# State space stage of an even layer: wide rotations by pairs of tiles, sums on TensorE, gates ahead of the attention heads, output projection between them

## The chip, the cores and the metric

The kernel runs on one core of a Trainium2 chip. The metric is the device time in microseconds (us). Before the change it is 1637.96 us, the median of three runs (1635.64 to 1639.87). TensorE (PE in the profile, its weight loads PEld) multiplies matrices into PSUM, VectorE (DVE), ScalarE (ACT) and GpSimd (POOL) work element by element, and SyncE (SP) issues the weight transfers.

## The reference, cut to what matters

A first block of two layers (feed-forward, a mixer of three branches, feed-forward) is followed by a second block: an even layer and an odd layer. The change lies in the even layer. All data are float32, 256 tokens, width 1024.

```python
h = rms_norm(x, even_norm_g)
q, k, v, z_a, u, z_b = split(h @ even_w_in)           # 4 x 1024 and 2 x 512 columns
q, k = per-head rms_norm(q), per-head rms_norm(k)     # 8 heads of 128
o_a = stick_breaking_attention(q, k, v) * silu(z_a)
o_b = s5_mixer(u, ...) * silu(z_b)
x = x + concatenate([o_a, o_b]) @ even_w_out          # 1536 x 1024

def s5_mixer(u):     # 32 groups of 16 channels, 64 complex states each
    bu = B_bar u                                      # real and imaginary
    h[t] = lam_bar h[t-1] + bu[t]                     # complex, diagonal
    y = C_re h.real - C_im h.imag + d u
    y = gelu(y)
    return y * sigmoid(y @ w_glu + b_glu)

def stick_breaking_attention(q, k, v):                # s < t
    z = q k / sqrt(128)
    w[t, s] = exp(log_sigmoid(z) + sum over s < j < t of (log_sigmoid(z) - z)[t, j])
    return w v
```

## The kernel before, in words

Activations lie transposed: 128 channels on the partitions, 256 tokens along the free axis (T = 256). Products of float32 matrices with weights are made in three parts: `W` (line 298 fetches, 311 and 312 split) takes a weight half of 128 x 1024, rounds it to a short form `wh` on ScalarE (L311) and has VectorE compute the rest `wl` (L312); `mm3` (L317 to L319) then multiplies wh x hi, wh x lo and wl x hi. `proj` runs that over the chunks of the contraction; for 1024 channels it is 24 matmuls of 256 columns. `tokens` gives token-major results in four steps of 12 matmuls of 512 columns each (L624 to L626). Two weight halves form a pair of 1 MB that one transfer on SyncE's queue brings; four buffers `raw` hold pairs, six buffers `hl` hold split halves.

`even` begins with the projection of u and the norm's factors. After that it holds three kinds of work. The first is a list `fills` of 36 closures: 24 token steps for v, q and k (the groups end in `heads`' norms, L1097 to L1102, and, three steps later, transposes, L1113), then twelve gates, 8 to 11 (z_b) ahead of 0 to 7 (z_a). `fill(x)` takes x of them on average, with the remainder carried over. Gates 8 to 11 get silu by a tanh at once, gates 0 to 7 by one activation after the last head (L1286).

The second is the state space part, 16 tiles of 128 states. `states(i)` makes the real and imaginary input products (L1160, L1161; 32 contraction rows, another group of 32 rows for each of four tiles) in one PSUM bank, then rotates them into the frame of the state: four VectorE products with the tables cos and sin (L1164, L1165, L1167, L1168) and two GpSimd sums (L1166, L1169). `rotate(i)` scans both parts along the tokens (L1177, L1178) and rotates back: two products on VectorE (L1180, L1183), two on GpSimd (L1181, L1184) and two GpSimd sums (L1182, L1185). `output(i)` makes two products with C (L1192, L1193; 32 output columns) into a quarter of one of two banks held for the whole part. `activated(c)` adds d u to four tiles' results and applies gelu. The loop runs over 18 steps with 1.4 fills each: `states(i + 1)`, `rotate(i)`, `output(i - 2)`. The GLU follows: four products of 12 matmuls.

The third is the attention: for each head `logits` (L1235), `remainder` (L1252) and `attend` (L1267), each with passes on ScalarE, VectorE and GpSimd between, one step apart over ten steps with one fill each. Then come silu of the z_a gates, the final norm's factor into new chunks (L1290), the product of heads and gates (L1294), and the output projection `out_rows`: twelve chunks of 24 matmuls, accumulated in four PSUM banks, added to h at the end (L1299).

The order on each engine is made by a scheduler ahead of the run from the order in which the code gives the work; buffers go back to their pools when all readers are done. PSUM has two banks each under the names a and b and four under c; temporaries have 12 buffers of 384 columns.

Of the kernel before, what the change touches and what calls it, by code (L numbers as in the profile page):

```python
# [9 lines left out]
F32 = mybir.dt.float32  # L10
# [20 lines left out]
# ---------------------------------------------------------------- host layout  # L31
# [204 lines left out]
# -------------------------------------------------------------------- kernel  # L236


class Kern:
    def __init__(self, ctx, tc, a, sizes, vwhere, cwhere):  # L240
# [7 lines left out]
        self.rawp = pool("raw", 4)  # L248
# [14 lines left out]
    # ---- small helpers  # L263
# [72 lines left out]
    def pair(self, n):  # L336
        """hi and lo accessors over n chunks of [P, T]."""
# [14 lines left out]
    def bcast(self, col, ps=None):  # L352
        """[P, 2] token columns -> [P, T] rows on every partition."""
# [13 lines left out]
    def token_sum(self, sq, st=None):  # L367
        """Columns [P, 2]: the sum of sq over partitions, per token."""
# [40 lines left out]
    def out_rows(self, tag, ks, ys, evac):  # L409
        """T-layout output, contraction chunk outermost; the last two by bank."""  # L410
        acc = [self.psc() for _ in range(4)]
        n = len(ks)
        done = {}
# [6 lines left out]
        for k in range(n - 2):  # L420
# [3 lines left out]
        ws = [self.W(tag + str(k)) for k in ks[n - 2:]]  # L424
        for b in range(4):
            for i in range(2):
                for d in (2 * b, 2 * b + 1):
                    blk(ws[i], n - 2 + i, d)
            for d in (2 * b, 2 * b + 1):
                evac(d, acc[b][:, (d % 2) * T:(d % 2) * T + T])  # L430
# [6 lines left out]
    # ---- parts  # L437
    def setup(self, x=True):
# [10 lines left out]
        # the tensor engine's clock rises while it works: it starts before the data come  # L449
# [10 lines left out]
    def setup_pos(self):  # L460
        """Distances and rotation tables from the positions: closures."""
# [6 lines left out]
        def fetch():  # L468
# [3 lines left out]
            pi = t["i"] = self.tp.tile([P, 384], I32, tag="t", name="posi")  # L472
# [31 lines left out]
    def reduce_angle(self, eng, y, x, k):  # L504
        """y = x - 2 pi round(x / 2 pi), within [-pi, pi]."""
# [7 lines left out]
    def ffn(self, part, l, h, extra=()):  # L513
# [13 lines left out]
        def project(f, *ups):  # L527
# [8 lines left out]
            # both at once: they follow the norm's chunks  # L536
# [53 lines left out]
    def small_norm(self, cks, g, n):  # L590
        """rmsnorm of T-layout chunks cks, then split."""
# [19 lines left out]
    def tokens(self, names, xs, sink, tag="a"):  # L611
        """Token-major [P, 512] per token block, contraction over 1024: four closures."""
# [44 lines left out]
    def pv(self, ptb, o, v, h):  # L657
        """o[qb][:, h*64:+64] = P @ v for both query blocks."""
# [6 lines left out]
    def attention(self, scores, pes, fill, pv, begun=0):  # L665
        """Scores, transposes and products of the eight heads, one stage apart."""
# [18 lines left out]
    def to_chunks(self, o, ys, scale=None):  # L685
        """token-major o [P, 2, 512] -> split T-layout chunks."""
# [11 lines left out]
    def mix(self, part, l, h):  # L698
# [10 lines left out]
        # latent attention: compressed inputs  # L709
# [16 lines left out]
        # differential attention inputs  # L726
# [17 lines left out]
        # lambda of the differential attention, on every partition  # L744
# [10 lines left out]
        # latent attention inputs  # L755
# [42 lines left out]
        def branch(n, c, ys):  # L798
            """Chunks c and c + 1 of branch n, gated, into the sum."""
# [64 lines left out]
        # latent attention  # L864
# [16 lines left out]
        # differential attention; o comes out times the first map's row sum  # L881
# [651 lines left out]
```

## Time and profile before

| what | before |
|---|---|
| median of three runs | 1637.96 us (1635.64 to 1639.87) |
| span of the profiled execution | 1638.3 us, mean granted TensorE clock 0.992 |
| TensorE busy, matmul / weight load | 1593.0 / 1501.5 us |
| VectorE / ScalarE / GpSimd busy | 1086.4 / 823.2 / 488.0 us |
| state space products on TensorE | first input product at 1280.67 us |
| attention heads | first logits at 1425.0 us |
| output projection of the even layer | last sum starts at 1506.6 us |

The busy time of an engine is the time in which at least one of its instructions runs; the records of matmuls overlap, so the busy time of weight loads says better how densely TensorE is fed. A group's line gives the count, the busy time, the mean of one instruction in ns, and the idle time ahead of it with what ended it.

### The profile page before, as it was taken

Reading aid. Unit: us, or ns where it says so; the run is one execution under the profiler, and the core shown is the slowest. Engines: PE = TensorE matmul, PEld = TensorE weight load, DVE = VectorE, ACT = ScalarE, POOL = GpSimd, SP = SyncE. Lnnn points to the kernel's source line nnn. Section 1 sums busy time; section 2 is a strip of 40 time slices with the busy share of each in tenths; the row PEclk is TensorE's granted clock in tenths of the full one; section 3 lists DMA queues with packets and bytes.
Section 4 is the critical chain, followed back from the end, with each engine's and each line's share of the span. In section 5 each row is a group of like instructions: output and inputs, shape, how many; then the busy total and the mean of one; then the engine's idle time right before and its main releaser. Section 6 shows DMA issues by size and latency. Waiting matters only on the chain.

```text
span 1638.3 us, 29940 instructions
## 1 busy us (share of the span) xinstructions
PE 1593.0 (97%) x12182; PEld 1501.5 (92%) x12182; DVE 1086.4 (66%) x1781; ACT 823.2 (50%) x1409; POOL 488.0 (30%) x539
## 2 busy tenths in 40 slices
PE   8999999999999999999999999999999989899998
PEld 8999998999999999999998999999999756789876
DVE  6655676676765557555576576776667899866642
ACT  5444455554544445444455564544545243575662
POOL 4111232003321113111142002455453678422232
PEclk9999999999999999999999999999999999999999
DMA  8555543344455554555544344554445322323520
GB/s 308 191 187 177 186 168 129 129 155 155 155 205 181 181 180 180 181 180 180 183 164 149 130 149 153 181 183 167 173 156 181 128 103 103 129 104 133 187 93 26
DMA packets 38313, 261.47 MB, mean 160 GB/s; under 512 B 4320, under 2 KB 5600, under 8 KB 7200
## 3 DMA queue, kind: packets, MB, share of 16 engines
q1 hardware_dynamic: 37440, 257.67, 44.4%
q8 instruction: 95, 1.56, 0.4%
q0 software_dynamic: 592, 1.81, 0.4%
q14 instruction: 42, 0.34, 0.1%
q10 hardware_dynamic: 144, 0.08, 0.0%
HBM read 258.50 MB, written 1.05 MB: 158 GB/s over the span
## 4 chain that ended last, share of the span: by engine, by line
PE 73%; DVE 13%; POOL 8%; issue 3%; ACT 3%; DMA 0%; SPq 0%; DVEq 0%; ACTq 0%; POOLq 0%
PE psa L317 11%; PE psa L318 11%; PE psa L319 11%; PE psc L318 6%; PE psc L319 6%; PE psc L317 6%; PE psb L317 5%; PE psb L318 4%; PE psb L319 4%; DVE wl L312 4%; POOL t L571 2%; POOL t L984 1%; ACT wh L311 1%; POOL t L822 1%; DVE s L334 1%
## 5 line engine op out<-in xcount | busy, mean ns | idle before, releaser
L312 DVE TENSOR_TENSOR wl<-raw,wh 128x1024 fp32r<-128x1024 f32 (+1 forms) x487 | 610.3, 1260 | 226.2 <-ACT wh L311 223.1
L311 ACT ACTIVATE wh<-raw 128x1024 fp32r<-128x1024 f32 (+1 forms) x487 | 505.8, 1049 | 423.0 <-PE psa L318 193.4
L317 PE MATMUL psa<-s,wh 128*128 128x256 f32 x1800 | 517.3, 288 | 1.4 <-ACT s L333 0.6
L318 PE MATMUL psa<-s,wh 128*128 128x256 f32 x1800 | 512.5, 285 | 3.9 <-DVE s L334 3.6
L319 PE MATMUL psa<-s,wl 128*128 128x256 f32 x1800 | 511.0, 284 | 0.0
L317 PEld LDWEIGHTS psa<-s,wh 128*128 128x128 f32 x1800 | 345.3, 192 | 11.1 <-issue 4.6
L318 PEld LDWEIGHTS psa<-s,wh 128*128 128x128 f32 x1800 | 345.5, 192 | 9.7 <-DVE s L334 7.8
L319 PEld LDWEIGHTS psa<-s,wl 128*128 128x128 f32 x1800 | 345.0, 192 | 2.2 <-issue 1.9
L571 POOL TENSOR_TENSOR t<-t,hrb 128x256 f32<-128x256 f32 x88 | 117.7, 1338 | 489.7 <-ACT t L570 489.7
L319 PE MATMUL psb<-s,wl 128*128 128x256 f32 x752 | 213.0, 283 | 1.1 <-DVE wl L312 1.1
L317 PE MATMUL psb<-s,wh 128*128 128x256 f32 x752 | 213.6, 284 | 0.0
L318 PE MATMUL psb<-s,wh 128*128 128x256 f32 x752 | 212.8, 283 | 0.0
L317 PE MATMUL psc<-hs,wh 128*128 128x256 f32 x704 | 198.7, 285 | 6.6 <-ACT hs L330 6.6
L318 PE MATMUL psc<-hs,wh 128*128 128x256 f32 x704 | 200.5, 286 | 1.5 <-DVE hs L331 1.0
L319 PE MATMUL psc<-hs,wl 128*128 128x256 f32 x704 | 199.2, 284 | 0.0
L319 PEld LDWEIGHTS psb<-s,wl 128*128 128x128 f32 x752 | 144.3, 192 | 1.5 <-DVE wl L312 1.5
L317 PEld LDWEIGHTS psb<-s,wh 128*128 128x128 f32 x752 | 144.3, 192 | 0.4 <-ACT t L1224 0.2
L318 PEld LDWEIGHTS psb<-s,wh 128*128 128x128 f32 x752 | 144.3, 192 | 0.0
L317 PEld LDWEIGHTS psc<-hs,wh 128*128 128x128 f32 x704 | 134.6, 192 | 8.3 <-ACT hs L330 8.2
L318 PEld LDWEIGHTS psc<-hs,wh 128*128 128x128 f32 x704 | 135.6, 193 | 3.5 <-DVE hs L331 3.5
L319 PEld LDWEIGHTS psc<-hs,wl 128*128 128x128 f32 x704 | 135.6, 193 | 0.0
L330 ACT ACTIVATE hs<-t 128x256 fp32r<-128x256 f32 x88 | 36.7, 417 | 156.0 <-DVE t L572 155.9
(366 smaller groups left out, 2323.6 us busy)
## 6 DMA issues: line engine op xcount, KB each, us to landing
raw<-in_w SPq DMA_DIRECT2D x242, 1024.0 KB, 4.8
s<-in_x SPq DMA_DIRECT2D x4, 256.0 KB, 5.1
raw<-in_w SPq DMA_DIRECT2D x4, 256.0 KB, 5.7
out<-t SPq DMA_DIRECT2D x8, 128.0 KB, 1.8
cst<-in_cst SPq DMA_DIRECT2D x1, 609.5 KB, 12.5
sq<-in_pw POOLq DMA_DIRECT2D x2, 256.0 KB, 3.7
s<-in_s5b POOLq DMA_DIRECT2D x1, 512.0 KB, 3.7
s<-in_s5c POOLq DMA_DIRECT2D x1, 512.0 KB, 3.9
```

What stands on the lines that cost most here:

```text
L311: self.act = nc.scalar.activation(hi[:, s], src[:, s], AF.Copy)
L312: nc.vector.tensor_tensor(lo[:, s], src[:, s], hi[:, s].bitcast(F32), ALU.subtract)
L317: mm(ps, wh, xh, start=start, stop=False, skip_group_check=True)
L318: mm(ps, wh, xl, start=False, stop=False, skip_group_check=True)
L319: return mm(ps, wl, xh, start=False, stop=stop, skip_group_check=True)
L330: nc.scalar.activation(hi, src, AF.Copy)
L334: nc.vector.scalar_tensor_tensor(lo, src, scale, hi.bitcast(F32), ALU.mult, ALU.subtract)
L571: nc.gpsimd.tensor_tensor(sg, sg, hrb, ALU.mult)
L822: nc.gpsimd.tensor_tensor(dst[:, 16:16 + T], src[:, 16:16 + T], src[:, 16 - sh:16 - sh + T], ALU.add)
L984: g.tensor_tensor(u, u, w, ALU.subtract)
```

## The change

State space tiles go in pairs. `states(n)` makes the input products of two tiles in turn, in two banks; each tile's real and imaginary part are then multiplied as one operand of 512 columns by cos and by sin, so two VectorE products take the place of four; the two GpSimd sums stay, in place. `rotate(n)` scans in place and makes two products of 512 columns on VectorE; the four GpSimd operations go. `output(n)` makes four products per tile instead of two, with a negated copy of the first matrix (`cneg`, made once in the preparation), so that TensorE's accumulation does the sums; the two tiles of a pair alternate. The loop has ten steps with 2 x 1.6 fills. All gates get silu by the tanh, and all fills left are done ahead of the GLU. The heads write into the projection's operands directly: the gate is multiplied on the way out of PSUM, the factor 0.5 is in the split. The final norm's factor is applied to h in place ahead of the heads. The output projection is cut into steps; they stand between the heads, without one in the loop's step 3. Its accumulators are the four banks c, and the heads' products use banks a and b. For the wider temporaries (512 columns) the weight buffers `raw` go from four to three, for the whole kernel.

```diff
-        self.rawp = pool("raw", 4)
+        self.rawp = pool("raw", 3)
...
-        t = self.tp.tile([P, 384], dt, tag="t", name="t")
+        t = self.tp.tile([P, 512], dt, tag="t", name="t")
...
+    def out_steps(self, tag, ks, ys, evac):
...
+        def step(k):
+            if not acc:
+                acc.extend(self.psc() for _ in range(4))
             w = self.W(tag + str(ks[k]))
             for d in range(8):
                 blk(w, k, d)
...
+            cn = self.const.tile([P, 16, 32], F32, name="cneg")
+            g.tensor_scalar(cn, c0[:, 0], -1.0, None, ALU.mult)
+            self.cp = c0[:, 0], c0[:, 1], cn
...
-            if c >= 8:
-                t = self.tmp()
-                nc.scalar.activation(t, z, AF.Tanh, scale=0.5)
-                nc.vector.scalar_tensor_tensor(z, t, 1.0, z, ALU.add, ALU.mult)
+            t = self.tmp()
+            nc.scalar.activation(t, z, AF.Tanh, scale=0.5)
+            nc.vector.scalar_tensor_tensor(z, t, 1.0, z, ALU.add, ALU.mult)
...
+        def states(n):
+            ii = (2 * n, 2 * n + 1)
+            pb = [self.psc() for _ in ii]
+            for m in range(2):
+                for i, ps in zip(ii, pb):
+                    r = slice(32 * (i % 4), 32 * (i % 4) + 32)
+                    nc.tensor.matmul(ps[:, m * T:m * T + T], bm[r, i // 4, m], u[r, i // 4],
+                                     start=True, stop=True)
+            for i, ps in zip(ii, pb):
+                gc, gs = self.tmp(512), self.tmp(512)
+                nc.vector.tensor_tensor(pairs(gc), pairs(ps), table(self.cos(i)), ALU.mult)
+                nc.vector.tensor_tensor(pairs(gs), pairs(ps), table(self.sin(i)), ALU.mult)
+                nc.gpsimd.tensor_tensor(gc[:, 0:T], gc[:, 0:T], gs[:, T:512], ALU.add)
+                nc.gpsimd.tensor_tensor(gc[:, T:512], gc[:, T:512], gs[:, 0:T], ALU.subtract)
+                hst[i] = gc, gs
+
+        def rotate(n):
+            for i in (2 * n, 2 * n + 1):
+                gc, gs = hst[i]
+                rho = self.rho[:, i:i + 1].to_broadcast([P, T])
+                for s in (slice(0, T), slice(T, 512)):
+                    nc.vector.tensor_tensor_scan(gc[:, s], rho, gc[:, s], 0.0, ALU.mult, ALU.add)
+                nc.vector.tensor_tensor(pairs(gs), pairs(gc), table(self.sin(i)), ALU.mult)
+                nc.vector.tensor_tensor(pairs(gc), pairs(gc), table(self.cos(i)), ALU.mult)
+
+        def output(n):
+            cr, ci, cn = self.cp
+            c = n // 2
+            for k, (m, src, half) in enumerate(((cr, 0, 0), (ci, 0, 1), (ci, 1, 0), (cn, 1, 1))):
+                for i in (2 * n, 2 * n + 1):
+                    o = yps[c % 2][32 * (i % 4):32 * (i % 4) + 32, (c // 2) * T:(c // 2) * T + T]
+                    nc.tensor.matmul(o, m[:, i], hst[i][src][:, half * T:half * T + T],
+                                     start=k == 0, stop=k == 3, skip_group_check=True)
...
+        for n in range(10):
+            fill(1.6)
+            if n < 7:
+                states(n + 1)
+            fill(1.6)
+            if n < 8:
+                rotate(n)
+            if 0 < n < 9:
+                output(n - 1)
+            if n > 1 and n % 2 == 0:
+                activated(n // 2 - 1)
...
+        fill(len(fills))
+        for c in range(4):
+            glu(c)
...
-            pz = self.psc()
+            pz = self.psa("a")
...
-            pr = self.psc()
+            pr = self.psa("b")
...
-            nc.scalar.activation(oa[hd // 4][:, hd % 4], po[:, 0:T], AF.Copy)
+            t = self.tmp()
+            nc.vector.tensor_tensor(t, po[:, 0:T], za[hd // 4][:, hd % 4], ALU.mult)
+            ys = ysa[hd // 4]
+            self.split(ys[0](hd % 4), ys[1](hd % 4), t, scale=0.5)
...
+        rfb = self.bcast(rf, self.psa("b", T))
+        for k in range(8):
+            nc.vector.scalar_tensor_tensor(h(k), h(k), self.v("final_norm", k), rfb, ALU.mult, ALU.mult)
...
-        for hd in range(10):
-            fill(1.0)
+        for hd in range(9):
             if hd < 7:
                 logits(hd + 1)
+            if len(steps) > 1 and hd != 3:
+                steps.pop()()
             if hd < 8:
                 remainder(hd)
+            if len(steps) > 1 and hd > 3:
+                steps.pop()()
-            if 0 < hd < 9:
+            if hd > 0:
                 attend(hd - 1)
```

## Rows read from the trace of the kernel before

**Rows 1.** The page: busy us, share of the span, instructions.

```profile
PE 1593.0 (97%) x12182; PEld 1501.5 (92%) x12182; DVE 1086.4 (66%) x1781; ACT 823.2 (50%) x1409; POOL 488.0 (30%) x539
```

**Rows 2.** Busy time by stage: stretch, its length, busy us (instructions), clock, DMA.

```profile
core 0: us, PE busy (x) PEld busy (x) DVE busy (x) ACT busy (x) POOL busy (x), PEclk, DMA share, GB/s
1282.00:1410.00 128.00, 115.19 (x472) 77.88 (x471) 121.22 (x178) 46.21 (x99) 105.99 (x103) 0.95 0.27 94
1475.00:1490.00 15.00, 15.00 (x127) 15.00 (x127) 10.94 (x13) 7.78 (x11) 3.15 (x4) 1.00 0.38 141
```

**Rows 3.** Groups by line, 1282 to 1410 us, VectorE: busy us, mean ns.

```profile
L312 DVE TENSOR_TENSOR wl<-raw,wh 128x1024 fp32r<-128x1024 f32 x24 | 38.3, 1634 | 0.0
...
L1183 DVE TENSOR_TENSOR t<-t,s 128x256 f32<-128x256 f32 x16 | 14.1, 878 | 0.0
...
L1164 DVE TENSOR_TENSOR t<-psc,s 128x256 f32<-128x256 f32 x16 | 6.6, 412 | 2.0 <-PE psc L1161 2.0
...
L1102 DVE TENSOR_TENSOR sq<-psa,sm 128x512 f32<-128x512 f32 x4 | 2.7, 684 | 0.1
```

**Rows 4.** The same view, 1410 to 1515 us, VectorE and ScalarE.

```profile
L312 DVE TENSOR_TENSOR wl<-raw,wh 128x1024 fp32r<-128x1024 f32 x26 | 31.5, 1224 | 15.7 <-ACT wh L311 15.6
...
L1241 ACT ACTIVATE t<-t,cst 128x384 f32<-128x384 f32 x8 | 4.9, 614 | 0.2
```

**Rows 5.** VectorE and GpSimd in order of time: start us, duration us, instruction.

```profile
1293.25 0.68 DVE L1177 TENSOR_TENSOR_SCAN t<-s5p,t 128x256 f32<-128x256 f32 x1
1293.85 1.16 DVE L1178 TENSOR_TENSOR_SCAN t<-s5p,t 128x256 f32<-128x256 f32 x1
...
1300.78 0.72 POOL L1166 TENSOR_TENSOR t<-t 128x256 f32<-128x256 f32 x1
...
1304.87 1.71 POOL L1182 TENSOR_TENSOR t<-t 128x256 f32<-128x256 f32 x1
...
1305.91 0.41 DVE L1164 TENSOR_TENSOR t<-psc,s 128x256 f32<-128x256 f32 x1
1306.25 0.41 DVE L1165 TENSOR_TENSOR t<-psc,s 128x256 f32<-128x256 f32 x1
...
1310.15 1.75 DVE L312 TENSOR_TENSOR wl<-raw,wh 128x1024 fp32r<-128x1024 f32 x1
1311.83 0.41 DVE L1164 TENSOR_TENSOR t<-psc,s 128x256 f32<-128x256 f32 x1
```

**Rows 6.** One line's instructions: ns min/median/max, first and last start.

```profile
L1183 DVE TENSOR_TENSOR t<-t,s x16: 413/948/965, 1289.4 to 1402.5; 128x256 f32<-128x256 f32 x16
```

**Rows 7.** TensorE in order of time, state space stretch.

```profile
1279.21 0.39 PE L624 MATMUL psb<-wh,s 128*128 128x512 f32 x1
...
1279.89 0.39 PE L624 MATMUL psb<-wh,s 128*128 128x512 f32 x1
...
1280.67 0.69 PE L1160 MATMUL psc<-s 32*128 32x256 f32 x2
1281.20 0.59 PE L1161 MATMUL psc<-s 32*128 32x256 f32 x2
...
1296.46 0.62 PE L1192 MATMUL psc<-t,s 128*32 128x256 f32 x2
...
1297.44 0.50 PE L624 MATMUL psa<-wh,s 128*128 128x512 f32 x1
```

**Rows 8.** TensorE in order of time, differential attention of the first layer.

```profile
366.01 0.61 PE L646 MATMUL psb<-s 32*128 32x256 f32 x4
```

**Rows 9.** Weight buffers: two stretches in order of time, and all fetches' landing.

```profile
444.62 5.16 DVE L312 TENSOR_TENSOR wl<-raw,wh 128x1024 fp32r<-128x1024 f32 x4
...
451.93 1.06 ACT L311 ACTIVATE wh<-raw 128x1024 fp32r<-128x1024 f32 x1 [2.25 <-PE psb L318]
...
DMA to landing us min/median/max: 4.0/4.8/11.6
```

**Rows 10.** One line's instructions, first logits and last sums.

```profile
L1235 PE MATMUL psc<-s x16: 377/379/383, 1425.0 to 1462.0; 128*128 128x256 f32 x16
...
L1299 DVE TENSOR_TENSOR s<-psc,s x8: 407/414/425, 1502.1 to 1506.6; 128x256 f32<-128x256 f32 x8
```

More of the change, by code (lines that the diff above doesn't have):

```diff
@@ L409, in out_rows @@
     def out_rows(self, tag, ks, ys, evac):
-        acc = [self.psc() for _ in range(4)]
+        for f in self.out_steps(tag, ks, ys, evac):
+            f()
+    def out_steps(self, tag, ks, ys, evac):
+        acc = []
         n = len(ks)
-        done = {}
         def blk(w, k, d):
@@ L423, in out_rows, with last @@
                 blk(w, k, d)
-        ws = [self.W(tag + str(k)) for k in ks[n - 2:]]
-        for b in range(4):
-            for i in range(2):
+        def last():
+            ws = [self.W(tag + str(k)) for k in ks[n - 2:]]
+            for b in range(4):
+                for i in range(2):
+                    for d in (2 * b, 2 * b + 1):
+                        blk(ws[i], n - 2 + i, d)
                 for d in (2 * b, 2 * b + 1):
-                    blk(ws[i], n - 2 + i, d)
-            for d in (2 * b, 2 * b + 1):
-                evac(d, acc[b][:, (d % 2) * T:(d % 2) * T + T])
+                    evac(d, acc[b][:, (d % 2) * T:(d % 2) * T + T])
+        return [lambda k=k: step(k) for k in range(n - 2)] + [last]
     def table_set(self, name):
@@ L1188, in output, with pairs @@
-        def output(i):
-            hr, hi = hst.pop(i)
-            c = i // 4
-            o = yps[c % 2][32 * (i % 4):32 * (i % 4) + 32, (c // 2) * T:(c // 2) * T + T]
-            nc.tensor.matmul(o, self.cp[:, 0, i], hr, start=True, stop=False, skip_group_check=True)
-            nc.tensor.matmul(o, self.cp[:, 1, i], hi, start=False, stop=True, skip_group_check=True)
-        y1, ysp, ysb = self.slot(), self.pair(4), self.pair(4)
+        def pairs(t):
+            return t.rearrange("p (m t) -> p m t", m=2)
@@ new lines, in table @@
+        def table(t):
+            return t.unsqueeze(1).to_broadcast([P, 2, T])
+        def states(n):
[13 more added lines that the diff above has]
+                hst[i] = gc, gs
@@ L1197, in activated @@
+        y1, ysp, ysb = u, self.pair(4), self.pair(4)
         def activated(c):
@@ L1256, in remainder @@
             wt = self.tmp(384)
[L1257 removed]
+            nc.scalar.activation(wt, lb, AF.Exp)
             for s in (0, T):
@@ L1270, in attend @@
                              skip_group_check=True)
[L1271 removed]
+            t = self.tmp()
[5 more added lines that the diff above has]
+            nc.vector.scalar_tensor_tensor(h(k), h(k), self.v("final_norm", k), rfb, ALU.mult, ALU.mult)
+        ys = [lambda k, j=j: ysa[k // 4][j](k % 4) if k < 8 else ysb[j](k - 8) for j in range(2)]
+        steps = self.out_steps("eo", [8, 9, 10, 11, 0, 1, 2, 3, 4, 5, 6, 7], ys,
+                               lambda d, ps: nc.vector.tensor_tensor(h(d), ps, h(d), ALU.add))
+        steps.reverse()
         with self.table_set("natural_log_exp_and_others")():
             logits(0)
[L1275 to L1276 removed]
+        for hd in range(9):
             if hd < 7:
                 logits(hd + 1)
+            if len(steps) > 1 and hd != 3:
+                steps.pop()()
             if hd < 8:
                 remainder(hd)
[L1281 removed]
+            if len(steps) > 1 and hd > 3:
+                steps.pop()()
+            if hd > 0:
                 attend(hd - 1)
[L1283 to L1300 removed]
+        while steps:
+            steps.pop()()
+        return h
     def odd(self, h, out):
```

78 lines of the change are left out of this document (9 added, 69 removed).

## The prediction

> **What bounds the kernel now.** I read the busy shares first: TensorE 97%, VectorE 66%, GpSimd 30% [rows 1]. These are averages over stages with different limits, so they decide nothing about a change in one stage. The change lies in one stretch, the even layer, so the next view is the table by stage. In a dense stretch (the output projection) 127 matmuls and 127 weight loads fill 15.00 us: 0.118 us each, TensorE is the bound. In the state space stretch, 1282 to 1410 us, the weight loads are busy 77.88 of 128 us while VectorE is busy 121.22 (95%) and GpSimd 105.99 [rows 2]: here VectorE is the bound, and TensorE waits for it. The groups by line say why. A split of a weight half (L312) takes 1634 ns here against 1224 ns after the stretch [rows 3, 4], and a rotation from SBUF (L1183) 878 ns, against 412 ns for a rotation of the same size that reads PSUM (L1164) [rows 3]. The instructions in order of time show the same: the four PSUM products follow one another at 0.34 us or a little less; the scans start 0.60 us apart when GpSimd is idle beside them; a split next to a GpSimd add takes 1.68 us from start to start [rows 5]. Tile after tile is 5.92 us (1305.91 to 1311.83), of which 1.68 are the split, so 4.24 are state space work [rows 5]. Check of the model: 16 x 4.24 + 24 splits x 1.634 + about 13 for the heads' norms and the rest = 120 us; from the end of the first input products at 1281.8 [rows 7] to that of the last rotation, which starts at 1402.5 [rows 6], there are 122. So VectorE's work, and nearly nothing else, makes this stretch.
>
> **The change part by part.**
>
> *State space on VectorE.* Undisturbed, a tile now costs 4 x 0.33 + 2 x 0.60 + 2 x 0.33 = 3.2 us; the measured 4.24 have 1.06 of disturbance by GpSimd, and a split has 0.41. Over the stretch that is 16 x 1.06 + 24 x 0.41 = 27 us beside 106 us of GpSimd work, about 0.26 us per us. After the change a tile has two wide products from PSUM, two scans and two wide products from SBUF. A 512-column product from PSUM is in the trace at 684 ns against 412 ns at 256 columns [rows 3], so 0.27 more: starts 0.60 us apart. A tile is then 4 x 0.60 + 2 x 0.60 = 3.6 us undisturbed, 0.4 more than now: the wide form folds eight products into four instructions, but two products come over from GpSimd. What pays is GpSimd's part: six operations per tile become two, 32 in all, of 0.72 us undisturbed and 1.71 beside a split [rows 5]: 23 us, with their own delays some 30. At 0.26 that disturbs VectorE by 8 us. Bounds: 0, if the adds fall beside the PSUM products, which are never slowed, and 23, if each add stops VectorE for its whole 0.72 us; 8 is taken since it is this kernel's own ratio.
>
> The trace shows mutual slowing, and no more than 0.5 us per split. The Trainium skill, page "SBUF — State Buffer", section "SBUF: two separate sides", states that the pair of ports is an exclusive lock, that a product with two SBUF inputs takes it against a GpSimd operation that reads SBUF, and that the loser blocks for the whole instruction. By that rule every add could cost VectorE its full time. The trace agrees that only products with two SBUF inputs suffer; the full block is rival 2 below.
>
> *Pace of the fills.* The eight pairs take 1 + 16 x 1.6 = 26 fills (24 token steps and two gates) instead of 24. VectorE's sum for that stretch: state space 57.6, disturbance 8, splits 26 x 1.15 = 30, norms of the heads and the rest 12 (13 now, less disturbance): 108 us. For the hand-overs between two engines that are nearly equally loaded I add 5 us (estimate, from the 122 against 120 above, doubled and a little more since TensorE is now close behind): 113 us. The stretch then ends at 1281.8 + 113 = 1395.
>
> *TensorE in that stretch.* A token step is 12 matmuls; three take 0.68 us, so 2.72. The two input products of a tile take 2 x 0.53 us, the two output products 0.98 [rows 7]. The change sets the products of two tiles side by side on different 32-row groups. The trace has that: in the differential attention two 32-row products of 256 columns, four records, have 0.61 us together [rows 8], where one product, two records, has 0.59 [rows 7]. So two tiles' input products cost what one costs now: 8 x 1.06 = 8.5 us against 17. The output products double (64 instead of 32), in pairs on different 32-column groups. No row shows column groups; from below a pair costs one product (then 8 x 2 = 16 us, no change), from above two (31 us). I take the lower, by the row-group row, the nearest. The Trainium skill, "TensorE: Matmul & The Clock Gate", Part 3, gives 2.38 times for three column tiles; no run here shows it. Sum: 24 x 2.72 + 2 x 2.83 + 8.5 + 16 + transposes 4 = 99 us, below VectorE's 113; with serial columns 115.
>
> *Gates.* All twelve gates now stand ahead of the heads. A gate is 24 matmuls, 2.83 us of TensorE [rows 2]; its two VectorE products of 0.33 and its 1.15 split fit beside that. Ten are left after 1395: 28.3, then the last output products 2 and the four GLU products of 12 matmuls, 5.7: heads begin at 1431. The eight silu gates by tanh save one activation table; ScalarE is not the bound there (46.21 of 128 us [rows 2]), so nothing.
>
> *Heads and output projection.* Now the heads begin at 1425.0 and the last sum starts at 1506.6 and takes 0.41, together 82 us [rows 10]. Eight gates (22.6) go out; 59.4 us remain, of which 34 are the projection's 288 matmuls and 25.4 the heads with their waits. The change puts the projection between the heads as fill in the place of the gates. It also takes the accumulators' four banks from the heads, leaving two and two; sets eight products with the final norm (256 columns from PSUM, 0.33 each or a little more, VectorE) at the beginning of the heads; leaves head 3 without a step; and ends on a chain from the last head through VectorE and ScalarE to the last products. For the gain of removing the wait before the projection (silu, products, splits) and for these new waits I have no row that tells them apart: from -4 to +6 us, taken as 0. So 59.4 remain and the layer ends at 1490.4 instead of 1507.0: **16.6 us earlier**.
>
> *Three weight buffers instead of four*, in the whole kernel. A pair is fetched when the third last is split, not the fourth last. The tightest place I found: four splits begin at 444.62 and last 5.16 us, the last three 1.14 each, so the first, which frees the buffer, ends near 446.4; the conversion that needs it begins at 451.93, 5.5 us later; a fetch lands in 4.8 us at the median, 11.6 at most, the long ones while everything is fetched at the start [rows 9]. So nothing; if a few collide, up to 2 us. The waiting fetch has only fetches behind it on its queue. The copy of one 512-column matrix that GpSimd writes in the preparation lies in front of GpSimd's product of the feed-forward stage; 0 to 1.2 us, taken as 0. Wider temporaries cost space alone, but a pair holds four of twelve and three pairs are in flight, so a head's squares may wait for output products; that is in the 5 us.
>
> **Sum.** 1638.3 (span of the profiled execution, and the median is 1638.0) - 16 = **1622 us**.
>
> **The rivals.**
> 1. *Output products on column groups run one after the other.* TensorE needs 115 us in the stretch, VectorE 108: TensorE leads, with the same 5 us, 120 instead of 113. 1629 us. For it: no row shows column groups. Against: row groups do overlap.
> 2. *Each GpSimd add blocks VectorE in full.* 23 us instead of 8: the gain falls to about 1 us, 1637 us. For it: a GpSimd add stretches from 0.72 to 1.71 us beside a split [rows 5], so the two do exclude each other. Against: the present ratio is 0.26.
> 3. *The heads' chain is laid bare: slower.* A head has four ScalarE passes over 384 columns of up to 0.61 us [rows 4], three VectorE passes that lie between the 0.41 and 0.68 of 256 and 512 columns [rows 3], 0.55, and six products of 1280 columns in all, 2.5 us at 0.49 per 256 [rows 7]: 6.6 us. If the fewer banks and the projection's weight splits, queued ahead on ScalarE and VectorE, leave all of it uncovered, heads and projection take 8 x 6.6 + 34 = 87 us and not 59.4: 27.6 lost against 16.6 won, 1649 us. It decides where each head waits 2.1 us longer than now. Against: today's heads cover most of it with one fill each.
> 4. *Everything fits.* Adds disturb nothing (-8) and nothing is lost between the engines (-5): 100 us beside TensorE's 99, 1609 us.
>
> **How the numbers follow.** Forecast 0.52, its own range 1614 to 1630; rival 1 0.16; rival 2 0.14; rival 3 0.10; rival 4 0.08. The range 1611 to 1637 takes in the bounds of the disturbance, the column groups and the heads' -4 to +6; rival 3 and the far half of rival 4 lie outside. A measurement of this kernel tells about 0.3%, 4.9 us, from no change. Faster than 1633: forecast, rivals 1 and 4, less a little of rival 1: 0.74. Same: rival 2 and that little: 0.16. Slower: rival 3: 0.10.
>
> **What would show it.** VectorE's splits in the stretch near 1.3 us instead of 1634 ns; GpSimd busy about 30 instead of 106 us; scans near 0.6 to 0.7 us; input products of two tiles starting within hundredths of a microsecond, and the same or not for the output products (rival 1); heads from about 1431 on; no wait of ScalarE on a weight fetch. The prediction is wrong if VectorE is idle often in the stretch (buffers, not work, then set the pace), or if head follows head later than 6 us.

## The result, and the profile after

The changed kernel takes 1622.7 us (median of four runs, 1621.3 to 1623.9) against 1638.3 for the kernel before (1635.6 to 1639.9): a ratio of 0.990, 95% interval 0.989 to 0.992. The forecast was 1622. The profiled execution has a span of 1619.9 us where the one before had 1638.3.

Busy time of the whole execution (us, share of the span, instructions):

```profile
PE 1577.3 (97%) x12246; PEld 1494.9 (92%) x12246; DVE 1073.3 (66%) x1765; ACT 820.3 (51%) x1406; POOL 416.2 (26%) x468
```

Beside [rows 1] GpSimd lost 72 us and the shares of the other engines moved by a point at most: the averages say as little about the change after it as before it. The table by stage says more: state space stretch, gates and GLU, heads and projection.

```profile
core 0: us, PE busy (x) PEld busy (x) DVE busy (x) ACT busy (x) POOL busy (x), PEclk, DMA share, GB/s
1285.00:1388.00 103.00, 91.27 (x449) 64.61 (x448) 96.99 (x139) 42.24 (x87) 35.70 (x38) 0.95 0.30 112
1388.00:1433.00 45.00, 45.00 (x370) 42.48 (x370) 32.06 (x54) 24.63 (x51) 3.60 (x3) 1.00 0.47 167
1433.00:1490.00 57.00, 56.14 (x409) 51.44 (x408) 41.86 (x80) 36.11 (x68) 9.95 (x32) 1.00 0.35 128
```

VectorE is still what leads the first stage (97 of 103 us, 94%, where [rows 2] has 95%), and TensorE follows it closely (91 us); in the other two TensorE is never idle for long. The groups of VectorE in the first stage (busy us, mean ns of one | idle before, releaser), and the two groups of GpSimd that are left of six:

```profile
L1194 DVE TENSOR_TENSOR_SCAN t<-s5p,t 128x256 f32<-128x256 f32 x32 | 27.4, 893 | 0.0
L312 DVE TENSOR_TENSOR wl<-raw,wh 128x1024 fp32r<-128x1024 f32 x20 | 24.7, 1260 | 0.7 <-ACT wh L311 0.7
L1196 DVE TENSOR_TENSOR t<-t,s 128x512 f32<-128x512 f32 x16 | 11.6, 724 | 0.0
L1195 DVE TENSOR_TENSOR t<-t,s 128x512 f32<-128x512 f32 x16 | 11.1, 694 | 0.0
L1184 DVE TENSOR_TENSOR t<-psc,s 128x512 f32<-128x512 f32 x16 | 10.9, 681 | 0.0
...
L1186 POOL TENSOR_TENSOR t<-t 128x256 f32<-128x256 f32 x16 | 15.0, 938 | 0.0
L1185 POOL TENSOR_TENSOR t<-t 128x256 f32<-128x256 f32 x16 | 14.6, 914 | 43.3 <-DVE t L1184 40.9 <-DVE sm L349 2.4
```

A split (L312) is back at 1260 ns from the 1634 of [rows 3]. The kernel before has these splits and scans in the stretch up to its last rotation, and one wait of VectorE for GpSimd that will matter too (its groups, 1281 to 1403 us):

```profile
L312 DVE TENSOR_TENSOR wl<-raw,wh 128x1024 fp32r<-128x1024 f32 x20 | 32.0, 1636 | 0.0
L1178 DVE TENSOR_TENSOR_SCAN t<-s5p,t 128x256 f32<-128x256 f32 x16 | 18.0, 1123 | 0.0
...
L1177 DVE TENSOR_TENSOR_SCAN t<-s5p,t 128x256 f32<-128x256 f32 x16 | 13.8, 861 | 0.0
...
L1100 DVE TENSOR_SCALAR sm<-sm 128x4 f32<-128x4 f32 x6 | 2.8, 462 | 5.4 <-POOL sm L350 5.4
```

Twenty splits before and twenty after: that count will matter below. The products of two tiles on TensorE (ns min/median/max, first and last start; first the input products of a pair, then the output products of a pair):

```profile
L1179 PE MATMUL psc<-s x8: 374/374/478, 1283.9 to 1284.6; 32*128 32x256 f32 x8
...
L1205 PE MATMUL psc<-t,s x12: 379/379/403, 1304.1 to 1305.2; 128*32 128x256 f32 x12
...
L1205 PE MATMUL psc<-t,cneg x4: 379/379/379, 1305.4 to 1305.6; 128*32 128x256 f32 x4
```

Eight records of two tiles' input products start within 0.7 us, and sixteen of the output products within 1.5: first start to last end is 1.1 and 1.9 us for a pair. The heads and the end of the layer (first logits, last sums):

```profile
L1254 PE MATMUL psa<-s x16: 377/380/456, 1433.0 to 1470.4; 128*128 128x256 f32 x16
...
L1302 DVE TENSOR_TENSOR s<-psc,s x8: 414/418/425, 1486.5 to 1489.8; 128x256 f32<-128x256 f32 x8
```

**Where the time came from.** From the first input products to the end of the last sum the layer took 226.3 us (1280.7 [rows 7] to 1507.0 [rows 10]) and takes 206.4 (1283.9 to 1490.2): 20.0 won. It begins 3.2 later, which takes that off again, so the layer ends 16.8 earlier. Of these 3.2, compared at the weight splits of VectorE in both traces, 0.3 stand there long before the layer, 1.5 come in the preparation (the experiment on the copy below) and 1.5 with the granted clock: between 1258 and 1264 us it fell in this execution and not in that of the kernel before (first before, then after):

```profile
1258.00:1264.00 6.00, 6.00 (x54) 6.00 (x52) 5.32 (x14) 4.65 (x12) 0.00 (x0) 1.00 0.55 182
...
1258.00:1264.00 6.00, 5.36 (x30) 5.17 (x31) 3.13 (x7) 3.27 (x8) 0.00 (x0) 0.72 0.62 221
```

Compared split by split in the same way (the n-th split of one trace with the n-th of the other), the odd layer then starts 15.4 earlier, so 1.4 go at the hand-over, and the last split stands 18.4 earlier. Those last 3.0 have nothing to do with the change: in the odd layer of the kernel before the granted clock stood at the lower of its two levels (1.2 GHz) for 6.8 us (1601.3 to 1608.2), behind 6.3 us in which TensorE was busy for 4.7; in this execution TensorE was busy for 4.4 of the 6.0 us at that place and the clock stayed up. The same ten microseconds of that layer in the kernel before, in the changed one, and in one of the experiments (cols_serial, whose edit lies in the even layer alone):

```profile
1600.00:1610.00 10.00, 10.00 (x41) 6.46 (x42) 2.31 (x7) 4.74 (x16) 4.94 (x10) 0.66 0.00 0
...
1584.60:1594.60 10.00, 9.99 (x57) 6.88 (x58) 4.15 (x9) 6.45 (x19) 5.59 (x11) 1.00 0.01 2
...
1585.00:1595.00 10.00, 10.00 (x40) 6.25 (x41) 2.31 (x7) 4.75 (x16) 4.94 (x10) 0.66 0.01 2
```

The third line has the code of the second in this layer and the clock of the first. So 20.0 - 3.2 - 1.4 + 3.0 = 18.4 between the two profiles; the medians, 15.5 apart, agree with what is left when the 3.0 are taken off.

### The profile page after: what moved, and what is told of

Its sections match the earlier page's. It is cut to its first block, busy times and chain, and to the rows that moved or that the text cites. A ratio compares the mean times of both kernels' runs of the same rounds, so it can differ in the third digit from the quotient of the medians.

```text
span 1619.9 us, 29923 instructions
## 1 busy us (share of the span) xinstructions
PE 1577.3 (97%) x12246; PEld 1494.9 (92%) x12246; DVE 1073.3 (66%) x1765; ACT 820.3 (51%) x1406; POOL 416.2 (26%) x468
## 4 chain that ended last, share of the span: by engine, by line
PE 73%; DVE 11%; POOL 9%; ACT 3%; issue 3%; DMA 0%; SPq 0%; DVEq 0%; ACTq 0%; POOLq 0%
PE psa L317 11%; PE psa L318 11%; PE psa L319 11%; PE psc L318 6%; PE psc L319 5%; PE psc L317 5%; PE psb L317 4%; PE psb L318 4%; PE psb L319 4%; DVE wl L312 2%; POOL t L581 2%; POOL t L994 2%; DVE t L1194 1%; ACT wh L311 1%; POOL t L832 1%
## 5 line engine op out<-in xcount | busy, mean ns | idle before, releaser
L312 DVE TENSOR_TENSOR wl<-raw,wh 128x1024 fp32r<-128x1024 f32 (+1 forms) x487 | 601.8, 1242 | 215.5 <-ACT wh L311 214.6
```

What stands on the lines that cost most here:

```text
L312: nc.vector.tensor_tensor(lo[:, s], src[:, s], hi[:, s].bitcast(F32), ALU.subtract)
```

## The experiments

**What the pairs are worth: the old tiles in the new order.** The states, rotate and output functions of the kernel before were put back, the rest left:

```diff
-        for n in range(10):
-            fill(1.6)
...
+        for i in range(18):
+            fill(1.78)
+            if i < 15:
+                states(i + 1)
...
```

> The changed kernel with the single-tile state space work of the kernel before put back (six GpSimd operations per tile, products of 256 columns, two output products per tile); gates, heads, projection and fetch buffers as in the changed kernel, and the fills between the tiles set so that as many token steps and gates lie in the stretch. My theory: VectorE's work in the stretch is again 16 x 4.24 + 26 x 1.634 + 13 = 123 us, 20 more than now, and TensorE has no work that could fill it elsewhere, so 1638 to 1645 us: all of the gain is the tiles'. Rival: the gain is that of the gates put inside and of the projection between the heads, so 1623 to 1630 us.

1640.0 us, a ratio of 1.001 (0.9996 to 1.002) to the kernel before. The new order without the new tiles brings nothing; the tiles bring 17.3 us in it. How much they bring without it is another question (tiles_only below).

**What GpSimd costs VectorE: none of its additions, and three times as many.**

```diff
-                nc.gpsimd.tensor_tensor(gc[:, 0:T], gc[:, 0:T], gs[:, T:512], ALU.add)
-                nc.gpsimd.tensor_tensor(gc[:, T:512], gc[:, T:512], gs[:, 0:T], ALU.subtract)
```

> The changed kernel without the 32 GpSimd additions, so the sums of the rotated inputs are left out of the result and of the work. My theory: VectorE loses its 8 us of disturbance, but TensorE has 99 us of work in a stretch of 102.5, so only 2 to 5 us are won, 1618 to 1621 us. Rival (each addition blocks VectorE in full, 23 us): the splits and scans lose far more, VectorE's busy time falls by over 20 us, and TensorE alone sets the stretch, 1612 to 1617 us.

1611.6 us, 11.1 won: more than I expected. VectorE's groups (state space stretch), and the stage:

```profile
L1192 DVE TENSOR_TENSOR_SCAN t<-s5p,t 128x256 f32<-128x256 f32 x32 | 20.3, 674 | 0.0
...
L312 DVE TENSOR_TENSOR wl<-raw,wh 128x1024 fp32r<-128x1024 f32 x21 | 25.2, 1218 | 1.3 <-ACT wh L311 1.3
L1183 DVE TENSOR_TENSOR t<-psc,s 128x512 f32<-128x512 f32 x16 | 10.9, 682 | 0.4 <-PE psc L1179 0.4
...
L1193 DVE TENSOR_TENSOR t<-t,s 128x512 f32<-128x512 f32 x16 | 10.8, 675 | 0.0
...
1285.00:1378.00 93.00, 89.35 (x452) 64.24 (x451) 87.25 (x140) 42.57 (x88) 6.95 (x6) 0.98 0.33 121
```

So 32 scans lose 219 ns each to the additions (7.0 us), the 32 products from SBUF 19 and 50 (1.1), 20 splits about 40 (0.8), the products from PSUM nothing: 8.9 us, for 29.6 us of GpSimd. My 2 to 5 failed on TensorE: I had set 99 us of its work into the stretch, but it is busy for 91 there in the changed kernel, so it gave way by more. That is an argument, not a measurement: between the 8.9 and the 11.1 the granted clock differs too (0.98 in this stage, 0.95 in the changed kernel's), and no run tells the two apart. For the other direction, 64 additions more:

```diff
+                for k in range(4):
+                    nc.gpsimd.tensor_tensor(self.scr, self.scr if k else gs[:, 0:T], self.scr, ALU.add)
```

> The changed kernel with 64 extra GpSimd additions of 256 columns, four behind the sums of each state tile, on a buffer that nothing else reads; the first of the four now reads that tile's product, since in more_pool the scheduler had put all 64 at the start of the kernel (2.5 to 65.7 us), where they delayed GpSimd's preparation by 32 us and said nothing on this stretch. 0.72 us each there, 46 us. My theory, from the kernel without additions (11.1 us won for 23 us of undisturbed work, 0.35 to 0.48 per us): 16 to 22 us more, 1638 to 1645 us, splits and scans slower. Rival, the prediction's 0.26: 12 us, 1633 to 1636 us. Second rival (an addition blocks VectorE in full): 46 us or more, 1665 us and above.

1650.0 us: 27.3 more than the changed kernel, between my figure and the full block. From the first product to the last rotation it is 128.3 us instead of 101.3. VectorE and GpSimd there, the longest wait of VectorE (us in total, times, longest), and the stage:

```profile
L1199 DVE TENSOR_TENSOR_SCAN t<-s5p,t 128x256 f32<-128x256 f32 x32 | 34.6, 1101 | 8.3 <-POOL t L1188 8.3
L312 DVE TENSOR_TENSOR wl<-raw,wh 128x1024 fp32r<-128x1024 f32 x20 | 26.3, 1337 | 0.7 <-ACT wh L311 0.7
L1200 DVE TENSOR_TENSOR t<-t,s 128x512 f32<-128x512 f32 x16 | 17.0, 1063 | 0.0
L1201 DVE TENSOR_TENSOR t<-t,s 128x512 f32<-128x512 f32 x16 | 14.3, 893 | 0.0
L1187 DVE TENSOR_TENSOR t<-psc,s 128x512 f32<-128x512 f32 x16 | 10.9, 678 | 0.0
...
L1191 POOL TENSOR_TENSOR scr<-scr 128x256 f32<-128x256 f32 x48 | 40.3, 839 | 3.3
L1191 POOL TENSOR_TENSOR scr<-t,scr 128x256 f32<-128x256 f32 x16 | 17.3, 1082 | 0.0
...
DVE t L1199 <- POOL t L1188: 8.3, 7, 1.8
```

Beside the changed kernel the scans lose another 6.7 us, the products from SBUF 8.6, the splits 1.5: 16.8 for 57.6 us of added GpSimd time, 0.29 per us. Most of the remaining price is another mechanism: VectorE waits 8.3 us for sums that stand behind the extra additions. With the run before, 8.9 / 29.6 = 0.30: the two directions agree. On the average that is far from 1, and the prediction's price for a full block, 0.72 us for each addition, is refuted by both runs: 0.28 us for each of 32, 0.26 for each of 64.

The single operations say more than the average. First the scans of the changed kernel (ns min/median/max, first and last start), then VectorE and GpSimd in order of time in the kernel with 64 additions more (start us, duration us):

```profile
L1194 DVE TENSOR_TENSOR_SCAN t<-s5p,t x32: 659/684/1226, 1288.6 to 1385.4; 128x256 f32<-128x256 f32 x32
...
1320.13 1.08 DVE L1199 TENSOR_TENSOR_SCAN t<-s5p,t 128x256 f32<-128x256 f32 x1 [0.56 <-POOL t L1188]
...
1320.63 1.12 POOL L1189 TENSOR_TENSOR t<-t 128x256 f32<-128x256 f32 x1
...
1321.14 1.16 DVE L1200 TENSOR_TENSOR t<-t,s 128x512 f32<-128x512 f32 x1
...
1321.70 1.18 POOL L1191 TENSOR_TENSOR scr<-t,scr 128x256 f32<-128x256 f32 x1
```

The durations of the scans fall into two groups with little between: in the changed kernel 17 of 32 take 0.66 to 0.69 us, as without additions, and 13 take 1.14 to 1.23. Where both engines have work, as in the last four lines, they take turns: each starts 0.50 to 0.56 us behind the other and lasts 0.4 to 0.5 us longer than alone (0.68 and 0.72). That is what an exclusive lock looks like, as the Trainium skill states it ("SBUF — State Buffer", section "SBUF: two separate sides"): the trace agrees with the rule, and not with the price that the prediction took from it. VectorE loses about 0.5 us where it comes second; where GpSimd comes second, GpSimd waits (1.11 us beside a scan, 1.71 beside a split, 0.72 alone); and beside a product from PSUM nobody waits, for these products stay at 678 to 682 ns in all three kernels. The 0.3 is the average of these cases in this kernel.

**Column groups.** First the four output products of a tile were issued behind one another:

```diff
-            for k, (m, src, half) in enumerate(((cr, 0, 0), (ci, 0, 1), (ci, 1, 0), (cn, 1, 1))):
-                for i in (2 * n, 2 * n + 1):
+            for i in (2 * n, 2 * n + 1):
+                for k, (m, src, half) in enumerate(((cr, 0, 0), (ci, 0, 1), (ci, 1, 0), (cn, 1, 1))):
```

> The changed kernel, with the four output products of one state tile issued before the four of the other, so that neighbours in the queue share their 32-column group and cannot overlap; the work is the same. My theory: the pairs of column groups overlap now, 16 us of TensorE in the stretch; one after the other they take 31, TensorE has 115 us of work in a stretch of 102.5, and the kernel takes 1628 to 1635 us. Rival: TensorE's order hardly matters since VectorE leads the stretch, 1623 to 1625 us.

1623.2 us, no change. The trace shows why it is no test of serial columns: the second tile's products began 0.9 us behind the first's and ran beside the rest of them (whether the scheduler or TensorE set that order no row tells), and a pair took 2.8 us (first start to last end) instead of 1.9.

```profile
L1205 PE MATMUL psc<-t,s x12: 379/379/404, 1303.5 to 1305.5; 128*32 128x256 f32 x12
...
L1205 PE MATMUL psc<-t,cneg x4: 379/379/379, 1304.9 to 1306.0; 128*32 128x256 f32 x4
...
1285.00:1388.00 103.00, 94.90 (x453) 67.47 (x452) 97.08 (x140) 42.59 (x88) 35.68 (x38) 0.98 0.30 110
```

TensorE was busy for 3.6 us more in the stretch, though the granted clock was higher there (0.98 against 0.95), and all of it was hidden behind VectorE. So the two tiles were set half a pair apart:

```diff
             fill(1.6)
+            if n > 1:
+                output(n - 2, 2 * n - 3)
...
             if 0 < n < 9:
-                output(n - 1)
+                output(n - 1, 2 * n - 2)
```

> The changed kernel, with the output products of a pair's two tiles half a pair apart, token steps between them; the work is the same. In cols_serial they still overlapped for the greater part (a pair took 2.8 us from the first start to the last end, against 1.9 in the changed kernel). My theory: now each tile's four take 1.7 to 2 us alone, 28 to 31 us in the stretch where they take 15 to 16, and TensorE, with 101 us of busy time in the 113 that hold the stretch, can take about 8 of the 13 to 15 us more: 1627 to 1632 us. Rival: VectorE leads by enough to hide all of it, 1622 to 1625 us; second rival, the prediction's serial sum, 1629 to 1636 us.

1627.6 us, 4.9 more. One tile's eight records, and the two stages up to the first logits:

```profile
L1205 PE MATMUL psc<-t,s x6: 379/379/403, 1317.1 to 1318.2; 128*32 128x256 f32 x6
...
L1205 PE MATMUL psc<-t,cneg x2: 379/379/379, 1318.4 to 1318.6; 128*32 128x256 f32 x2
...
1285.00:1388.00 103.00, 98.61 (x453) 68.72 (x452) 97.54 (x138) 43.33 (x90) 38.34 (x38) 0.98 0.31 110
1388.00:1437.00 49.00, 49.00 (x366) 43.10 (x365) 32.07 (x55) 23.56 (x47) 2.59 (x3) 1.00 0.44 155
```

A tile alone takes 1.9 us, exactly what the pair takes together; 8 x 1.9 = 15 us more for TensorE. The last rotation came only 0.5 us later than in the changed kernel, the heads 3.9 later: the price is paid in the stage behind, where TensorE is the bound.

**The order of heads and projection.** All steps of the projection were given behind the heads:

```diff
-            if len(steps) > 1 and hd != 3:
-                steps.pop()()
...
-            if len(steps) > 1 and hd > 3:
-                steps.pop()()
```

> The changed kernel, with all of the output projection behind the stick-breaking heads instead of between them. My theory, that of the prediction's rival on the heads turned round: without fill each head shows its chain of ScalarE and VectorE passes, two heads in flight hide part of it, and the kernel loses 8 to 16 us, 1631 to 1639 us. Rival (the prediction's zero for the interleaving): the heads overlap among themselves and the order is worth nothing, 1621 to 1625 us.

1624.9 us (ratio to before 0.9905 to 0.994): no change, but again no test. The scheduler, not the code, sets the queue, and it filled the heads with projection products all the same. So the projection's matmuls were tied behind the last matmul of the last head:

```diff
+        with self.tc.issue_after(self.last_po.ins):
+            while steps:
+                steps.pop()()
```

> The changed kernel, with every matmul of the output projection tied behind the last matmul of the last head; in proj_after the scheduler still put projection products between the heads. My theory: bare heads hide only part of one another; a head's chain is 6.6 us by the prediction, two are in flight, so 8 heads take 35 to 45 us instead of the 25 of TensorE time, and the kernel takes 1632 to 1642 us. Rival: heads and projection cost the same in any order, as the prediction's zero for the interleaving assumed, 1622 to 1625 us.

1642.9 us: 20.2 more. TensorE in the 41 us from the first logits on, in proj_after and then in this kernel, and its longest wait there:

```profile
1433.00:1474.00 41.00, 39.30 (x272) 35.00 (x271) 31.82 (x61) 28.42 (x52) 9.96 (x30) 1.00 0.30 109
...
1433.00:1474.00 41.00, 23.39 (x114) 17.86 (x112) 27.49 (x58) 23.47 (x47) 8.59 (x32) 0.92 0.13 48
...
PE psa L1254 <- DVE t L1262: 14.7, 6, 6.8
```

Bare heads take 41 us, and the next head's logits wait 14.7 us for VectorE to have read the bank that they need. With projection products between them the same 41 us hold 39 to 40 of TensorE work.

**The tiles alone.** The gates were left between the heads (as tanh), and the projection tied behind them as in proj_pin:

```diff
-            fill(1.6)
+            fill(1.36)
...
-        fill(len(fills))
         for c in range(4):
             glu(c)
...
         for hd in range(9):
+            fill(1.0)
```

> The changed kernel with the state tiles in pairs, but with the gates and the projection about where the kernel before has them: 24 instead of 26 fills by the last rotation, eight of the twelve gates between the heads (as tanh, as in the changed kernel), and the output projection tied behind the last head. My theory: moving gates and projection is neutral, as the prediction had it, and the tiles alone bring the gain, 1620 to 1626 us. Rival: the order of the later part brings a third or more, 1627 to 1634 us.

1665.4 us, far outside both. One of ScalarE's two groups of table loads between the first logits and the end of the heads (the other, on L1275, has the same numbers), and the stage:

```profile
L1259 ACT ACT_TABLE_LOAD x7 | 9.0, 1283 | 0.1
...
1414.00:1498.00 84.00, 57.79 (x312) 51.82 (x311) 43.05 (x83) 53.27 (x78) 10.21 (x32) 0.82 0.18 62
```

A tanh between the heads' exponentials and logarithms costs two table loads of 1283 ns, 18 us of ScalarE's time in all, and TensorE works 58 of 84 us, at a granted clock of 0.82; the tied projection alone had cost 20.2 in proj_pin. The run doesn't price the tiles without the new order, which stays open; it shows a dependence: gates that use tanh at once are dear between the heads, which speaks for moving them ahead of the heads if silu is made that way.

**The preparation and the copy.** With GpSimd's copy of the negated matrix written at the start of the even layer:

```diff
             cn = self.const.tile([P, 16, 32], F32, name="cneg")
-            g.tensor_scalar(cn, c0[:, 0], -1.0, None, ALU.mult)
...
         gg = self.const.tile([P, 8], F32, name="gfe")
+        nc.gpsimd.tensor_scalar(cn, self.c0[:, 0], -1.0, None, ALU.mult)
```

> The changed kernel, with GpSimd's copy of the negated matrix moved from the preparation to the start of the even layer, where GpSimd has nothing to do. My theory: in the preparation the copy (1.49 us) stands ahead of GpSimd's product of the feed-forward stage, which VectorE waits for, and the start of the even layer moved by 3 to 4 us because of it; without it there 1619 to 1620 us, and the weight splits of the stretch before the even layer come within 1.5 us of those of the kernel before. Rival: the delay has other causes (the granted clock fell there in this run), so 1622 to 1623 us as the changed kernel.

1624.3 us, no change, and the copy began at 1242.2 us, where it had been: the scheduler had taken it forward. Tied behind the first sums instead:

```diff
+            if n == 0:
+                with self.tc.issue_after(last.ins):
+                    cn = self.const.tile([P, 16, 32], F32, name="cneg")
+                    nc.gpsimd.tensor_scalar(cn, self.c0[:, 0], -1.0, None, ALU.mult)
```

> The changed kernel, with the copy of the negated matrix tied behind the first GpSimd additions of the even layer; in cneg_late the scheduler had put it at the same place as before (it began at 1242.18 us against 1242.48), so that run said nothing on the copy. My theory: the copy costs the preparation the 1.45 us by which the weight splits move at the 398th, and nothing behind it; the median comes 1 to 2 us below the changed kernel, 1620 to 1622 us, and the splits from the 398th on stand within 0.5 us of those of the kernel before until the granted clock falls. Rival: the copy also causes the 1 to 2 us more that show up to the 404th, and 1618 to 1620 us. Second rival: the delay is not the copy's, 1622 to 1624 us.

1619.1 us, a ratio to the kernel before of 0.987 (0.985 to 0.990): the best of the kernels here that leave no work out. VectorE's wait in the preparation (1240 to 1250 us), in the changed kernel and in this one:

```profile
DVE t L582 <- POOL t L581: 6.2, 1, 6.2
...
DVE t L582 <- POOL t L581: 4.7, 1, 4.7
```

The 1.5 us step at the 398th split is gone and everything behind it stands 1.5 earlier, so the copy was the cause, and of that much alone. The medians differ by 3.6, but the two profiled executions, both with a mean granted clock of 0.994, by 1.4 alone; the other three of this kernel have 0.996 and are its shortest, so the other 2 go along with the clock, and no kept row tells more of them.

**Three fetch buffers.**

```diff
-        self.rawp = pool("raw", 4)
+        self.rawp = pool("raw", 3)
```

> The kernel before with three weight fetch buffers instead of four and nothing else. My theory: the fetches are still early enough everywhere, so the time stays that of before, 1638 us, within 2. Rival: in the trace of the changed kernel ScalarE waited 8.6 us for two fetches in the state space stretch; if such waits cost what they last, this kernel takes 1643 to 1650 us.

1640.2 us, ratio 1.0006 (0.999 to 1.002): no cost that can be told from zero. Its splits stand 0.5 us behind those of the kernel before up to 1258 us and 2.0 behind from 1276 us to the end: nothing is lost in all the stages between but 1.5 us where the granted clock fell (0.72 from 1258 to 1264 us, as in the changed kernel). Whether chance or the three buffers brought that fall no run tells. In the changed kernel ScalarE does wait for fetches in the stretch (1285 to 1398 us):

```profile
ACT wh L311 <- DMA raw<-in_w: 8.6, 2, 6.0
```

but VectorE waits only 0.7 us for ScalarE's half of a split there (the L312 row above), so ScalarE's slack takes nearly all of it. (Three buffers alone were tried in the kernel before; the changed kernel was not tried with four.)

One run with extra additions that read nothing of the tiles tested nothing here: the scheduler put all 64 at the start of the kernel, and the 1656.4 us are the preparation's.

```diff
+                for _ in range(4):
+                    nc.gpsimd.tensor_tensor(self.scr, self.scr, self.scr, ALU.add)
```

> The changed kernel with 64 extra GpSimd additions of 256 columns on a buffer of its own that nobody reads, four behind the two of each state tile, about 46 us of GpSimd work undisturbed. My theory: GpSimd slows VectorE by 0.26 us for each us of its work, 12 us, in a stretch where VectorE is busy 105 of 113 us: 1631 to 1637 us. Rival (an addition blocks VectorE in full): 46 us or more, 1660 to 1670 us. Second rival (no disturbance): 1622 to 1624 us.

## Why the prediction was right, and where its steps were off

**The bound.** That VectorE makes the stretch, and that GpSimd makes VectorE slow, is shown from three sides: old tiles, no additions, more additions.

**Disturbance: 8 predicted, 8.9 measured**, and the ratio 0.26 is 0.30. For the kernel before the ratio stands: beside the same operations undisturbed (674 ns a scan, 1218 a split, 412 a product) its scans, splits and products on L1183 lost 26 us beside 101 us of GpSimd (1282 to 1403 us). By this account, which no run isolates, what the tiles won is disturbance that is gone (26 against 8.9 us) and not work: VectorE's own work in a tile grew, by 0.4 us in the prediction's sum. Rival 2 (full block, 23 us) falls with both runs as a price, not as a mechanism: the two engines do shut each other out, but GpSimd waits as well, and part of the additions falls beside products from PSUM. What is left of the disturbance showed up elsewhere than expected, on the scans and not on the splits, since the additions now run beside the scans.

**The stretch: 113 predicted, 102.6 measured** (from 1285.0, the end of the first input products, to the last rotation at 1387.6). The failed step is the number of splits: I counted 24 for the kernel before, from the window that ends at 1410 [rows 3], and 26 after; up to the last rotation there are 20 in either. Six splits too many are 7 us. The heads' norms, the rest and the coupling, 12 and 5 in the prediction, come to 13 (102.6 less 57.6, 8.9 and 20 x 1.15), and 6 of these are idle time of VectorE, 5.4 of it six waits for GpSimd in the heads' norms, as many as in the kernel before (L1100). The prediction's check of 120 against 122 us closed by luck: four splits from behind the last rotation, 6.5 us, stood in for waits that it didn't count. **Gates and GLU: 36 predicted, 45.4 measured**: what I had set into the stretch too much came back behind it, at TensorE's pace. The two errors have mainly one cause and nearly cancel (-10.4 and +9.4); with the later start that is why the heads, put at 1431, began at 1433. That this sum came out is luck.

**TensorE and the column groups.** The pair at the price of one product holds: 15 us for eight pairs against the 16 taken. Rival 1 falls for the order that was written; its price, 7 us, was near: 4.9 in cols_apart, which also sets half of the products half a pair later. Its place was wrong, since the stretch hid the work and the stage behind it paid. The Trainium skill ("TensorE: Matmul & The Clock Gate", Part 3) has 2.38 times for three column tiles; two tiles gave 3.8 / 1.9 = 2.0 times here.

**Heads and projection: 59.4 predicted, 57.2 measured.** The zero for the interleaving was right as a sum of two large terms: taking the gates out of the heads uncovers 20 us (proj_pin; rival 3 had 27.6), and the projection between them covers it again. Rival 3 named the right mechanism, and the condition on which it fails is the scheduler's: it fills a head's gaps with whatever is ready.

**The copy: 0 to 1.2 predicted, taken as 0; 1.5 measured.** This was the one cost outside its stated bounds. The row of its wait was there: VectorE waited for the GpSimd product behind it, so nothing covered it. The three buffers cost nothing that shows, as said; but the sign "no wait of ScalarE on a weight fetch" was wrong, with 8.6 us of such waits, which reached VectorE for 0.7.

**The sum.** The layer won 20.0 against 16.6 predicted, the preparation and the hand-over to the odd layer took 4.6, which the prediction had at 0 (1.5 of it the copy, 1.5 the granted clock before the layer; of the 1.4 at the hand-over no run tells the cause), and the clock in the odd layer gave the profile 3.0. The median came within 1 us of the forecast by errors that cancel, none above 11 us.

## What to carry to other kernels

Count the work that lies in a stretch between two events of the chain, not in a window that looks like it, and check the count on another row. Before an order in the code is priced, look whether a scheduler keeps it: two edits here left the order as it was in the main and a third put its work into another stage, and only tied instructions told what the order is worth. Fewer and wider operations on the engine that leads, with GpSimd's part given to TensorE by accumulation, paid even though VectorE took over work.

## What the runs showed of the hardware that was not expected

A GpSimd addition and a VectorE operation with both inputs in SBUF took turns here, whichever VectorE operation it was: about 0.5 us more for the one that came second on VectorE (a scan 0.68 and 1.16 us, a split 1.22 and 1.75), and 0.4 to 1.0 more for GpSimd (0.72 alone, 1.11 beside a scan, 1.71 beside a split); products from PSUM were not slowed at all. Over the stretch that made 0.3 us of VectorE's time per us of GpSimd's. Output products of one column group that stand in the code in front of another group's did not hold the other group up for all of their time: the pair took 2.8 us where 1.9 is the overlapped time and 3.8 the serial one. And the granted clock moved the time by 3 us between executions with the same code in the odd layer, which is as much as the smaller effects here.
